# Instance norm over rows of 4096: ScalarE takes the first row's mean of each tile in place, VectorE the other three

One core of one Trainium2 chip. The metric is device time in microseconds (us) of one execution; lower is better.

## The reference

```python
x: float32 [256, 256, 4096], eps = 1e-5
mean = np.mean(x, axis=2, keepdims=True)
var = np.var(x, axis=2, keepdims=True)
return ((x - mean) / np.sqrt(var + eps)).astype(np.float32)
```

There are 65,536 rows of 4096. Every byte is read once and written once: 2147.5 MB of traffic in all. The input is drawn from a standard normal distribution.

## The kernel before

A tile holds 128 partitions x 4 rows x 4096. Three tile buffers rotate. SyncE (SP) issues all transfers on one queue, VectorE (V) and ScalarE (A) compute. Per tile SP does this:

```python
def store(s, t):                       # cut to its core
    take(S, done[s], K + 1)            # 4 applies by V, 1 by A
    S.dma_start(out=..., in_=X[s][:, :, :]).then_inc(stored[s], 16)
def load(s, t, wait=True):
    take(S, stored[s], 16)             # the buffer's last store has landed
    S.dma_start(out=X[s][:, :, :], in_=...).then_inc(loaded[s], 16)
...
for t in range(L0, L0 + BUFS):         # in a loop over rounds
    store(t % BUFS, ...)               # tile t
    load((t + 2) % BUFS, ...)          # tile t + 2
```

VectorE divides each row by 4096 in place and sums it, which gives the mean; ScalarE squares `x/4096 - mean` (scaled back) into a scratch tile in PSUM (an on-chip memory) and sums the squares, then takes a square root for each pair of rows; VectorE applies scale and bias to the rows, with ScalarE taking three quarters of the last row:

```python
for r in range(r0, r0 + k):                                    # V, line 87
    V.tensor_scalar(out=x[:, r, :], in0=x[:, r, :], scalar1=1.0 / d, scalar2=None,
        op0=ALU.mult, op1=ALU.add, accum_out=mean[s][:, r : r + 1]).then_inc(means, 1)
...
for r in range(r0, last + 1):                                  # A, line 137
    if own: A.wait_ge(own_a, own)
    ...                                # wait until V has counted r - r0 + 1 means
    mine(A.activation(out=junk, in_=x[:, r, :], func=AF.Square, bias=mean[s][:, c],
        scale=-float(d), accum_out=ss[s][:, c]))
    ...                                # after rows 1 and 3: square root of two rows, line 146
```

The first and the last tile are handled in halves of two rows, so one tile function runs 130 times: 126 whole tiles and 4 halves.

## Time and profile before

| | before |
|---|---|
| median of the first three runs | 4963.04 us (4962.19 to 4963.28) |
| span of the profiled run | 4960.2 us |
| VectorE busy, ScalarE busy | 66%, 49% |
| period of a tile in mid-run | 38.66 us |
| C: a tile's landing to the end of its last apply | 26.2 us |

The costliest groups on the page (line, engine, operation, out<-in, count | busy us, mean ns of one | idle time just before and what ended it):

```profile
L87 DVE TENSOR_SCALAR_CACHE_REDUCE x<-x 128x4096 f32<-128x4096 f32 x512 | 2232.3, 4416 | 1580.4 <-DMA x<-in_x_dram 1580.4
L137 ACT ACTIVATE junk<-x,mean 128x4096 f32<-128x4096 f32 x512 | 1883.1, 3678 | 2367.2 <-DVE x L87 2367.2
```

The row sum on VectorE (L87) is the largest block of engine work, and ScalarE is idle half of the time, mostly waiting for it. The 1580.4 us before L87 are VectorE waiting for loads.

### The profile page before, as it was taken

To read this page: it belongs to the slowest core of one execution; us is meant where nothing else is said; L and a number is where in the kernel's file an instruction comes from. 1 tells how busy PE (TensorE), PEld (TensorE's weight loads), DVE (VectorE), ACT (ScalarE), POOL (GpSimd) and SP (SyncE) were. 2 spreads that over 40 slices of the span, in tenths; PEclk is the share of its full clock that TensorE was granted. 3 is DMA by queue.
4 is the path that set the end of the run, shared out by engine and by line. 5 is a ranking of instruction groups with operands and counts; after the bars stand their busy time and mean duration, and the time that the engine had idled before them with its cause. 6 is when DMAs were issued, how large, how long until landed. Compare 5 with 4: busy or idle time off the path is not lost.

```text
span 4960.2 us, 5938 instructions
## 1 busy us (share of the span) xinstructions
DVE 3298.0 (66%) x2049; ACT 2407.7 (49%) x1412; POOL 0.2 (0%) x4
## 2 busy tenths in 40 slices
DVE  6666666666666666666666666666666666666666
ACT  4455444554445544455445544455444554445544
POOL 0000000000000000000000000000000000000000
DMA  9999999999999999999999999999999999999999
GB/s 422 431 435 433 431 435 433 432 437 432 432 438 432 433 437 432 433 437 432 435 435 432 436 434 431 438 433 431 438 433 432 438 432 433 438 432 433 438 432 405
DMA packets 37298, 2147.52 MB, mean 433 GB/s; under 512 B 4144, under 2 KB 4144, under 8 KB 4144
## 3 DMA queue, kind: packets, MB, share of 16 engines
q1 hardware_dynamic: 37296, 2147.50, 100.0%
q14 instruction: 2, 0.02, 0.0%
HBM read 1073.74 MB, written 1073.74 MB: 433 GB/s over the span
## 4 chain that ended last, share of the span: by engine, by line
DVE 62%; another core or an unknown queue 31%; issue 4%; DMA 2%; ACT 0%; DVEq 0%; ACTq 0%; SPq 0%
DVE x L87 44%; DVE x L112 17%; DMA x<-in_x_dram 1%; DVE nbias L100 1%; DMA out_dram<-x 1%; DVE rstd L98 1%; ACT junk L137 0%; DVEq L68 0%; DVEq L219 0%; ACT L146 0%; ACT std L146 0%; ACTq L68 0%; ACTq L67 0%; SPq L265 0%
## 5 line engine op out<-in xcount | busy, mean ns | idle before, releaser
L87 DVE TENSOR_SCALAR_CACHE_REDUCE x<-x 128x4096 f32<-128x4096 f32 x512 | 2232.3, 4416 | 1580.4 <-DMA x<-in_x_dram 1580.4
L137 ACT ACTIVATE junk<-x,mean 128x4096 f32<-128x4096 f32 x512 | 1883.1, 3678 | 2367.2 <-DVE x L87 2367.2
L112 DVE TENSOR_SCALAR x<-x,rstd,nbias 128x4096 f32<-128x4096 f32 (+1 forms) x512 | 1004.2, 2004 | 33.9 <-DVE nbias L100 29.3
L151 ACT ACTIVATE x<-x,nbias,rstd 128x3072 f32<-128x3072 f32 x130 | 383.2, 2948 | 146.2 <-DVEq L68 146.2
L137 ACT ACTIVATION_READ_ACCUMULATOR junk<-x,mean 128x1 f32 x512 | 95.5, 187 | 0.0
L146 ACT ACTIVATE std<-ss,eps_tile 128x2 f32<-128x2 f32 x256 | 75.6, 295 | 19.1
L98 DVE RECIPROCAL rstd<-std 128x2 f32<-128x2 f32 x256 | 40.7, 159 | 19.4 <-ACT std L146 19.4
L100 DVE SCALAR_TENSOR_TENSOR nbias<-mean,rstd 128x2 f32<-128x2 f32 x256 | 41.1, 161 | 8.9
L87 DVE DVE_READ_ACCUMULATOR x<-x 128x1 f32 x512 | 42.3, 83 | 0.0
L137 ACT ACT_TABLE_LOAD x1 | 1.3, 1283 | 1.2 <-DVE eps_tile L216 1.2
L146 ACT ACT_TABLE_LOAD x1 | 1.3, 1283 | 0.1
L216 DVE MEMSET eps_tile<- 128x1 f32 x1 | 0.1, 59 | 1.0 <-SPq L192 1.0
L251 POOL MEMSET const-bfloat16-1.0<- 128x1 bf16 x1 | 0.1, 101 | 0.0
L251 POOL MEMSET const-uint8-127<- 128x1 uint8 x1 | 0.1, 101 | 0.0
L251 POOL MEMSET const-float32-1.0<- 128x1 f32 x1 | 0.1, 99 | 0.0
L251 POOL MEMSET const-float32-0.0<- 128x1 f32 x1 | 0.1, 98 | 0.2 <-issue 0.2
## 6 DMA issues: line engine op xcount, KB each, us to landing
out_dram<-x SPq DMA_DIRECT2D x4, 4096.0 KB, 19.6
x<-in_x_dram SPq DMA_DIRECT2D x2, 4096.0 KB, 16.7
x<-in_x_dram SPq DMA_DIRECT2D x127, 50.3
out_dram<-x SPq DMA_DIRECT2D x126, 31.5
```

The source lines that it names most:

```text
L87: V.tensor_scalar(out=x[:, r, :], in0=x[:, r, :], scalar1=1.0 / d, scalar2=None, op0=ALU.mult, op1=ALU.add, accum_out=mean[s][:, r : r + 1 ...
L98: mine(V.reciprocal(out=rstd[s][:, c], in_=std[s][:, c]))
L100: mine(V.scalar_tensor_tensor(out=nbias[s][:, c], in0=mean[s][:, c], scalar=-1.0 / d, in1=rstd[s][:, c], op0=ALU.mult, op1=ALU.mult))
L112: V.tensor_scalar(out=x[:, r, f], in0=x[:, r, f], scalar1=rstd[s][:, c], scalar2=nbias[s][:, c], op0=ALU.mult, op1=ALU.add,).then_inc(dn, 1)
L137: mine(A.activation(out=junk, in_=x[:, r, :], func=AF.Square, bias=mean[s][:, c], scale=-float(d), accum_out=ss[s][:, c]))
L146: A.activation(out=std[s][:, c], in_=ss[s][:, c], func=AF.Sqrt, bias=eps_tile, scale=1.0 / d**3).then_inc(stds, 1)
L151: A.activation(out=x[:, last, :Q], in_=x[:, last, :Q], func=AF.Identity, bias=nbias[s][:, c], scale=rstd[s][:, c]).then_inc(dn, 1)
L216: V.memset(eps_tile, eps / d**2).then_inc(ready, 1)
L251: nc = _bacc.Bacc("TRN2", target_bir_lowering=False, num_devices=1)
```

## The change

The intent: take the first of the four row sums off VectorE and give it to ScalarE, which starts it as soon as the tile lands. A new semaphore passes the landing on.

```diff
+    landed = nc.alloc_semaphore("landed")
...                                                  # vector_tile
-        for r in range(r0, r0 + k):
+        V.sem_inc(landed, 1)
+        for r in range(r0 + 1, r0 + k):
             V.tensor_scalar(...)
...                                                  # scalar_tile
+        take(A, landed, 1)
+        mine(A.activation(
+            out=x[:, r0, :], in_=x[:, r0, :], func=AF.Copy, scale=1.0 / d, accum_out=mean[s][:, r0 : r0 + 1]
+        ))
         for r in range(r0, last + 1):
             c = slice(r, r + 1)
-            if own:
-                A.wait_ge(own_a, own)
+            A.wait_ge(own_a, own)
             if r == last:
-                take(A, means, k)
-            else:
-                A.wait_ge(means, r - r0 + 1)
+                take(A, means, k - 1)
+            elif r > r0:
+                A.wait_ge(means, r - r0)
```

## The prediction

> **What bounds the kernel now.** I read the page's busy shares first, then its DMA lines, then the timeline of two tiles in mid-run with the issuing queue, then the waits, then stretches of mid-run. The busy shares and the traffic:
>
> ```profile
> DVE 3298.0 (66%) x2049; ACT 2407.7 (49%) x1412; POOL 0.2 (0%) x4
> DMA  9999999999999999999999999999999999999999
> HBM read 1073.74 MB, written 1073.74 MB: 433 GB/s over the span
> x<-in_x_dram SPq DMA_DIRECT2D x127, 50.3
> out_dram<-x SPq DMA_DIRECT2D x126, 31.5
> ```
>
> No engine is busy all the time; the DMA engines are, in every slice. A tile is 128 x 4 x 4096 x 4 B = 8.39 MB, so one transfer at 433 GB/s is 19.4 us and a load plus a store is 38.75 us. The timeline shows how a tile's period is filled (start, duration, engine, line; excerpts of one tile and the start of the next):
>
> ```profile
> 2408.09 4.42 DVE L87 TENSOR_SCALAR_CACHE_REDUCE x<-x 128x4096 f32<-128x4096 f32 x1 [12.55 <-DMA x<-in_x_dram]
> 2412.56 3.68 ACT L137 ACTIVATE junk<-x,mean 128x4096 f32<-128x4096 f32 x1 [17.17 <-DVE x L87]
> ...
> 2425.85 4.74 DVE L112 TENSOR_SCALAR x<-x,rstd,nbias 128x4096 f32<-128x4096 f32 x2
> ...
> 2431.07 2.95 ACT L151 ACTIVATE x<-x,nbias,rstd 128x3072 f32<-128x3072 f32 x1 [1.14 <-DVEq L68]
> 2431.16 3.13 DVE L112 TENSOR_SCALAR x<-x,rstd,nbias 128x4096 f32<-128x4096 f32 x2 [0.30 <-DVE nbias L100]
> 2434.53 0.34 SPq L165 DMA_DIRECT2D out_dram<-x  x1
> 2435.11 0.35 SPq L170 DMA_DIRECT2D x<-in_x_dram  x1
> 2446.75 4.42 DVE L87 TENSOR_SCALAR_CACHE_REDUCE x<-x 128x4096 f32<-128x4096 f32 x1 [12.46 <-DMA x<-in_x_dram]
> ```
>
> The period is 2446.75 - 2408.09 = 38.66 us: the transfer time of a tile's 16.78 MB, at 434 GB/s. Work from a tile's landing to its last apply takes C = 2434.29 - 2408.09 = 26.2 us; then both engines stand still some 12.5 us until the next load lands. The waits say the same:
>
> ```profile
> DVE x L87 <- DMA x<-in_x_dram: 1580.4, 126, 13.2
> DVE rstd L98 <- ACT std L146: 19.4, 4, 5.8
> ```
>
> 1580.4 / 126 = 12.5 us per tile. Is that wait a latency or a queue? Landing times decide. The store issued at 2434.53 lands 31.5 us later though it needs 19.3 us, and the load issued just behind it takes 50.3 us. That is 12.2 us of an older load still ahead, then 19.3 us for the store, then about 19 us for the load itself: work in a queue that is served in order and is never empty. So DMA is the bound, with roughly 12 us of queued work in hand when the next pair is issued. The chain of waits gives VectorE 62% of the span, but it walks back through engine work wherever that joins a load's arrival; it doesn't weigh that the load would not have come sooner.
>
> **What the Trainium skill says.** (1) "DMA: Bandwidth & Descriptors", section "Where 436 GB/s comes from": 16 ports x 32 B x 850 MHz = 435 GB/s is the ceiling of the path to SBUF. The trace agrees: 433 over the span, 434 in mid-run, so there is under half a per cent left to win. (2) "SBUF — State Buffer", section "SBUF: two separate sides": engine accesses and DMA use different ports and don't slow each other. Stretches of mid-run, cut at the ends of the engines' work, agree (length, DVE busy, ACT busy, POOL busy, clock, DMA share, GB/s):
>
> ```profile
> 2408.00:2434.50 26.50, 25.79 (x16) 18.74 (x11) 0.00 (x0) 1.00 0.99 430
> 2434.50:2446.70 12.20, 0.00 (x0) 0.00 (x0) 0.00 (x0) 1.00 1.02 440
> ```
>
> 430 GB/s with engines at work and 440 without; records are credited packet by packet, so 2% over 12 us is no finding. (3) "ScalarE: Activation LUTs", section "What ACT_TABLE_LOAD costs": an activation with immediate scale and bias takes 186 ns + 0.833 ns per element, and each per-partition operand adds about 93 ns. The trace agrees: the square (one such operand, 4096) would be 3.69 us and takes 3.68; L151 (two, 3072) would be 2.93 and takes 2.95. (4) The same page, "Table sets: the hidden batching unit": copy is in every table set, so the new operation needs no further table load. The kernel before has two loads of 1.28 us in the whole run although three functions alternate, which fits; its trace has no copy.
>
> **The change, part by part.** Each of 130 calls (126 full tiles, and 2 tiles in halves) moves its first row from VectorE to ScalarE.
>
> Removed on VectorE: 130 of 512 instructions of L87. One advances the engine by 4.34 us (from the first row's start at 2408.09 to the second's at 2412.44, in the timeline), 4.36 us of busy time each (2232.3 / 512). 130 x 4.36 = 567 us, plus 130 accumulator reads of 83 ns = 11 us: busy falls from 3298 to about 2720 us (55%).
>
> Added on ScalarE: 130 copies with accumulation. Estimate from the page just named: 186 + 0.833 x 4096 = 3.60 us, plus the 0.187 us accumulator read of L137. 130 x 3.79 = 492 us: busy rises from 2408 to about 2900 us (58%). A semaphore increment on VectorE passes the landing on, about 0.1 us.
>
> Moved: the chain inside a tile. Count from the landing. ScalarE: copy 0.1 to 3.8 (accumulator read included; it overlaps its activation by 0.07); square of row 0 from 3.9 to 7.7, of row 1 from 7.9 to 11.7 (3.80 each with its read), first square root to 12.0, squares of rows 2 and 3 from 12.2 to 20.0, second root to 20.4 (0.295 each, gaps 0.03 to 0.2 as in the trace). VectorE: three rows end at 3 x 4.34 = 13.0; reciprocal and bias to 13.5; two applies in 4.17 to 17.6; then it waits for the second root until 20.5, some 2.5 to 3 us that it didn't wait before; reciprocal, bias and start 0.55; last applies 3.13. New C = 24.2 us, 2.0 us less than 26.2. ScalarE now carries the tile's chain.
>
> What is this worth? The pair store(t), load(t+2) is issued 2.0 us earlier after the landing, into a queue with 12.2 us of work in hand. It then has 14.2 us in hand. The load still lands one period of 38.6 us after the one before. On the path that sets the end: 124 x 0 = 0. The load's own wait, for the store of the tile before, doesn't bite: that store was issued one period earlier, at about 2395.9, and landed at 2427.4, which is 19.3 us after the landing at 2408.1, and the load will be asked for at 24.4.
>
> Start and end: the first tile's halves come free about 1 us sooner each (17.0 to 16.0), but two loads of 19.3 us fill the queue to about 41 us and the first half-store was issued at 31.5. At the end the last half-store was issued at 4941.7 and would come some 4 us sooner (2.0 from the last full tile, 1 from each half). From 4952 to the end only the slower DMA engines still move data, 84 GB/s over 8.2 us; those had a backlog at 4941.7 and don't end sooner for an earlier issue. At best, if slow and fast engines share a resource, the 0.06 of DMA share missing between 4908 and 4942 returns: 2 us. Sum: 0 to -2 us of 4963. I choose -1: **4962 us**.
>
> **The rivals.**
> *The loop is a latency loop.* A load's landing, C, and the issue of the load two tiles on close a ring: 26.2 + 0.6 + 50.3 = 77.1 us = two periods of 38.6. If 50.3 us were fixed, a shorter C would take 1.0 us off each period: 4963 - 124 = 4839 us, 2.5% faster. If even the 12.5 us wait were fixed, 124 x 2.0 = 248 us: 4715. For it speaks only the chain of waits and that the sum closes; against it, 50.3 is explained as queueing and 434 GB/s leaves no room under the 435.
> *ScalarE becomes the bound.* It has 2900 / 130 = 22.3 us of work in a 38.6 us period. C would have to grow to 38 us to starve the queue; even a copy at twice my estimate gives about 28. Time: 4962 still. Only a wait that I overlook, of over 14 us a tile, would cost time; then each further microsecond costs 124 us.
> *Contention.* ScalarE now also writes 2 MB more per tile to SBUF, VectorE as much less. If the 430 against 440 GB/s were contention after all, summed engine busy time barely changes (25.8 + 18.7 to 21.4 + 22.5 us a tile), so under 0.2%: 4953 to 4972.
>
> **Range and chances.** The three runs lie within 1.1 us. I add the end effect (to -2 us), a possible shift of the DMA rate with issue order (0.1%, 5 us, either way): 4955 to 4968. The latency loop gets 1.5%; something that starves the queue 1%.
>
> **What would show it.** Right: DVE busy near 2720 and ACT near 2900 us; copies of about 3.6 us, 130 of them; C near 24.2; VectorE's wait for loads up to about 14.5 us a tile (1580 to some 1820 us); a new wait of L98 for the square root, 2.5 to 3 us a tile, 310 to 370 us in all; landings later by 2 us (store 33.5, load 52.3) with the period at 38.6 and 433 GB/s. Wrong: landings unchanged with a shorter period (latency loop), or VectorE's load wait gone and GB/s below 430 (starved).

## The result

Ratios in this document are the mean time of one kernel's fast runs over that of the other's fast runs of the same rounds, so not quite the ratio of the medians that are quoted.

The changed kernel takes **4965.26 us** (4964.86 to 4965.61, 6 runs) against 4963.06 us (4961.5 to 4963.66, 6 runs): ratio 1.0005, 95% interval 0.9992 to 1.0018. The same within 2%, and inside the range of 4955 to 4968.

The page after: busy shares, DMA share in 40 slices, and issues with KB where known and us from issue to landing.

```profile
DVE 2745.6 (55%) x1789; ACT 2875.9 (58%) x1672; POOL 0.2 (0%) x4
DMA  9999999999999999999999999999999999999999
x<-in_x_dram SPq DMA_DIRECT2D x127, 52.9
out_dram<-x SPq DMA_DIRECT2D x126, 34.2
```

VectorE gave 552 us away and ScalarE took on 468 us, DMA is as full as it was, and both landing times grew by 2.6 to 2.7 us. The groups that changed (columns as above):

```profile
L89 DVE TENSOR_SCALAR_CACHE_REDUCE x<-x 128x4096 f32<-128x4096 f32 x382 | 1668.2, 4417 | 1906.0 <-DMA x<-in_x_dram 1906.0
L132 ACT ACTIVATE x<-x 128x4096 f32<-128x4096 f32 x130 | 470.1, 3616 | 1915.2 <-DVEq L69 1915.2
L100 DVE RECIPROCAL rstd<-std 128x2 f32<-128x2 f32 x256 | 41.7, 163 | 249.4 <-ACT std L151 249.4
```

130 sums left L89; 130 copies of 3.616 us stand at L132. VectorE's wait for loads rose from 1580.4 to 1906.0 us: the time saved in each tile reappears as waiting for the next one. ScalarE's 1915.2 us are the same wait, passed on by VectorE's semaphore increment. One tile in mid-run (start, duration, engine, line; cut):

```profile
2406.88 4.42 DVE L89 TENSOR_SCALAR_CACHE_REDUCE x<-x 128x4096 f32<-128x4096 f32 x1 [15.09 <-DMA x<-in_x_dram]
2406.89 3.62 ACT L132 ACTIVATE x<-x 128x4096 f32<-128x4096 f32 x1 [15.26 <-DVEq L69]
...
2410.63 3.68 ACT L142 ACTIVATE junk<-x,mean 128x4096 f32<-128x4096 f32 x1
...
2420.30 4.73 DVE L114 TENSOR_SCALAR x<-x,rstd,nbias 128x4096 f32<-128x4096 f32 x2
...
2426.32 0.29 ACT L151 ACTIVATE std<-ss,eps_tile 128x2 f32<-128x2 f32 x1
2426.75 0.17 DVE L100 RECIPROCAL rstd<-std 128x2 f32<-128x2 f32 x1 [1.73 <-ACT std L151]
...
2427.30 3.14 DVE L114 TENSOR_SCALAR x<-x,rstd,nbias 128x4096 f32<-128x4096 f32 x2 [0.19 <-DVE nbias L102]
...
2430.68 0.34 SPq L170 DMA_DIRECT2D out_dram<-x  x1
2431.26 0.35 SPq L175 DMA_DIRECT2D x<-in_x_dram  x1
2445.52 4.42 DVE L89 TENSOR_SCALAR_CACHE_REDUCE x<-x 128x4096 f32<-128x4096 f32 x1 [15.08 <-DMA x<-in_x_dram]
```

C is now 2430.44 - 2406.88 = 23.56 us, 2.6 us less. The period is 2445.52 - 2406.88 = 38.64 us: unchanged. The engines wait 15.1 us for each load where they waited 12.5. VectorE now waits for the second square root of each tile, which it didn't before.

### The profile page after: what moved, and what is told of

Same layout as the page of the kernel before. It is cut to its first block, busy times and chain, and to the rows that moved or that the text cites. A ratio compares the mean times of both kernels' runs of the same rounds, so it can differ in the third digit from the quotient of the medians.

```text
span 4963.8 us, 6069 instructions
## 1 busy us (share of the span) xinstructions
DVE 2745.6 (55%) x1789; ACT 2875.9 (58%) x1672; POOL 0.2 (0%) x4
## 4 chain that ended last, share of the span: by engine, by line
another core or an unknown queue 38%; ACT 37%; issue 16%; DVE 7%; DMA 1%; DVEq 0%; ACTq 0%; SPq 0%
ACT junk L142 26%; ACT x L132 10%; DVE x L114 6%; ACT std L151 1%; DMA x<-in_x_dram 1%; DVE nbias L102 1%; DVE rstd L100 0%; DVEq L69 0%; ACTq L69 0%; DVEq L224 0%; ACT L151 0%; ACT L132 0%; ACT x L156 0%; SPq L186 0%
## 5 line engine op out<-in xcount | busy, mean ns | idle before, releaser
L89 DVE TENSOR_SCALAR_CACHE_REDUCE x<-x 128x4096 f32<-128x4096 f32 x382 | 1668.2, 4417 | 1906.0 <-DMA x<-in_x_dram 1906.0
L132 ACT ACTIVATE x<-x 128x4096 f32<-128x4096 f32 x130 | 470.1, 3616 | 1915.2 <-DVEq L69 1915.2
L100 DVE RECIPROCAL rstd<-std 128x2 f32<-128x2 f32 x256 | 41.7, 163 | 249.4 <-ACT std L151 249.4
L89 DVE DVE_READ_ACCUMULATOR x<-x 128x1 f32 x382 | 31.6, 83 | 0.0
L132 ACT ACTIVATION_READ_ACCUMULATOR x<-x 128x1 f32 x130 | 24.2, 187 | 0.0
## 6 DMA issues: line engine op xcount, KB each, us to landing
x<-in_x_dram SPq DMA_DIRECT2D x127, 52.9
out_dram<-x SPq DMA_DIRECT2D x126, 34.2
```

The lines of the kernel that those rows point to most:

```text
L100: mine(V.reciprocal(out=rstd[s][:, c], in_=std[s][:, c]))
L132: mine(A.activation(out=x[:, r0, :], in_=x[:, r0, :], func=AF.Copy, scale=1.0 / d, accum_out=mean[s][:, r0 : r0 + 1]))
```

## The experiments

"Before" is always the kernel before, on the same chip, in the same rounds; its medians were 4962.06 us (9 runs on chip 12, beside no arithmetic, the changed kernel again, and one and three more squares), 4962.11 (7 runs on chip 1, of which two took 4999 and 5002; beside five more squares and less traffic), 4962.55 (7 runs on chip 1; two more squares and three rows loaded) and 4962.48 (11 runs on chip 12; the split store). So two more squares ran on another chip than one, three and the split.

**Theory A**: DMA is the bound, its queue is never empty, and C only sets how much work still stands in it when the next transfer is issued (the work in hand). **Rival B**: the landing time is a fixed latency, and a shorter C shortens the loop. **Rival C**: engine accesses slow the DMA.

### 1. No arithmetic at all

```diff
 # vector_tile, after the wait for the load
-        for r in range(r0, r0 + k):
-            V.tensor_scalar(...)
-        ...
+        V.sem_inc(dn, k + 1)
 # scalar_tile is never called
```

> Loads, stores and their semaphores alone, no arithmetic (wrong result on purpose). Theory A, full queue (DMA is the bound, and a tile's compute time C only sets how much work is queued): with C near 0 still 4950 to 4970 us, period 38.6 us, landings longer (about 58 us for load and store). Theory B, latency loop (landing time is fixed near 50.3 us): period (0.3 + 0.6 + 50.3) / 2 = 25.6 us, about 3300 us. Theory C, contention (engine accesses slow the DMA from 440 to 430 GB/s): 440 GB/s throughout, about 4885 us.

Measured: 4959.61 us (4958.65 to 4962.99, 5 runs) against 4962.06, ratio 0.9996 (0.9983 to 1.001). (It counted as correct because the input is nearly normalised already; it is a copy and no solution.) The page:

```profile
DVE 0.1 (0%) x1; POOL 0.2 (0%) x4
HBM read 1073.74 MB, written 1073.74 MB: 433 GB/s over the span
x<-in_x_dram SPq DMA_DIRECT2D x127, 57.7
out_dram<-x SPq DMA_DIRECT2D x126, 57.6
```

With C at nothing the time stays and the landing of a load grows from 50.3 to 57.7 us and that of a store from 31.5 to 57.6: the landing time is queueing. (A load's grows less because SP now waits, before it issues one, for the store of the tile before: 2413.3 us in 129 waits.) B (3300 us) and C (4885 us) fall. Against C speaks a stretch of the changed kernel too: it shows 439 GB/s with the engines at work (2406.80 to 2430.70 us) and 425 without (2430.70 to 2445.50), the reverse of the 430 and 440 in the prediction. All 5700 us of engine work in the kernel before cost some 2.5 us of span, within the spread of the runs. So a change on the engines alone has no more than about that to gain here while all this traffic goes through this queue.

### 2. The changed kernel again

> The changed kernel once more, as a control on this chip. If the 2.2 us that it lost are the kernel's own, 4964.5 to 4966 against 4961.5 to 4964 for the kernel before; if they were chance of a chip or a day, the two overlap.

Measured: 4965.32 us (4964.72 to 4966.14, 5 runs) against 4962.06 (4961.19 to 4963.24). The two groups don't overlap, as in the first comparison, though the 95% interval of the ratio, 0.9992 to 1.002, includes 1. The loss of 2 to 3 us (some 0.06%) is small but comes back in a second set of runs, so it seems to belong to the kernel. More on it below.

### 3. Longer C: one, three and five more squares per tile

In each whole tile ScalarE repeats the square of row 0 into PSUM `n` times; the last one is overwritten with the same value, so the result stays right.

```diff
+        for _ in range(n if k == K else 0):
+            A.wait_ge(own_a, own)
+            mine(A.activation(out=junk, in_=x[:, r0, :], func=AF.Square, bias=mean[s][:, r0 : r0 + 1],
+                 scale=-float(d), accum_out=ss[s][:, r0 : r0 + 1]))
```

> The changed kernel with one more square of row 0 into PSUM per full tile: C from 23.6 to 27.4 us, a little over the kernel before (26.2), ScalarE's writes to SBUF unchanged. Theory A: same, 4960 to 4968. For the lost 2.2 us: if more work in hand costs them, about 4963 or less, as before; if ScalarE's added writes to SBUF cost them, still about 4965. Theory B: 1.9 us per period more, about 5205.

> Three more squares of row 0 per full tile: C about 35.1 us, 11.5 us more, still under the period of 38.6. Theory A: same, 4958 to 4970, and the engines' wait for loads falls from 15.1 to about 3.5 us a tile. Theory B: 5.8 us per period more, about 5690.

> Five more squares of row 0 per full tile: C about 42.8 us, over the 38.6 us period. Theory A: the queue runs dry and the engines set the pace: 126 x 42.8 us plus about 90 us at start and end, 5470 to 5500 us, DMA share near 0.9, no wait for loads left. Theory B: 9.6 us per period more, about 6175.

Measured: one more (C 27.4 us) 4964.23 us (4963.54 to 4975.24, 5 runs, four of them under 4965.5), ratio 1.001. Three more (C 35.1) **5055.88** us (5053.63 to 5069.38, 5 runs), ratio 1.0188 (1.0174 to 1.0202). Five more 5439.68 us (2 runs), ratio 1.0934 (1.0854 to 1.1014; the two slow runs of before are in its base).

The first is as A expects. The second is a miss: A promised 4958 to 4970 for every C under the period of 38.6, and B its 5690. The third is in the regime that A named, but 30 us under the range: the period is 42.44 us between store issues, not 42.8, because ScalarE goes straight from one tile into the next. The DMA queue's line (packets, MB, share of the 16 engines' span that packets took) and the traffic, with three more:

```profile
q1 hardware_dynamic: 37296, 2147.50, 99.3%
HBM read 1073.74 MB, written 1073.74 MB: 424 GB/s over the span
```

and with five more, with the busy shares:

```profile
DVE 2745.4 (50%) x1789; ACT 5256.6 (97%) x2932; POOL 0.2 (0%) x4
q1 hardware_dynamic: 37296, 2147.50, 93.2%
```

With five, ScalarE is the bound (97%) and the queue stands empty for part of each tile. With three, the queue is empty for only 0.7% of the span and still moves 2% less. The packet records of the trace say how. A packet of 64 KB takes 2.418 us in the median in all these kernels, but some take longer:

```
                      packets over 2.6 us   their excess over
kernel                (of 32,384)           2.418 us, per engine
before                  101                    3.4 us
changed                 150                    4.1
no arithmetic           114                    3.6
one more                155                    5.0
three more             1892                   67.2
five more              2503                  100.9
```

The long packets with three and five more lie almost all 16 to 24 us after a store's issue, where the queue turns from the store to the next load. The few of the kernel before lie mostly 6 to 10 us after the issue, where it turns from a load to the store; nearly half of them (46 of 101) fall in the first 250 us, and one after 1250. For the profiled run with three more (5069.38 us, 107 us over before) the sum nearly closes: 0.7% of 5067.6 us are 35 us of empty queue, and the long packets add 67.2 - 3.4 = 64 us. So the loss with three has two parts, and the slower packets are the larger.

The trace shows a second thing that A had overlooked. A load's landing is when the last of its 16 DMA engines is done. With three more, in one tile 15 engines reported between 2413.02 and 2413.38 us and the sixteenth at 2415.86. SP issued the next store at 2412.50, "3.4 us ahead of the landing", but the last packets of those 15 engines ended at 2412.7 to 2413.0, and their next ones started only at 2413.3. What the landing shows in hand is the last engine's work; the first engines have less, by the spread between them.

### 4. Where does the loss begin

Two more squares, and two with one of half a row:

```diff
-        for _ in range(n if k == K else 0):
+        for w in (d, d) if k == K else ():          # plus2h: (d, d, d // 2)
             ...                                      # the same on [:, :w]
```

> The changed kernel with two more squares of row 0: C about 31.2 us. Theory D (a queue with work has no cost, but it runs dry some 3 to 4 us before its last load's landing is seen, so the cliff lies near C = 34 us and not at the period of 38.6): 4960 to 4968 us, period 38.7. Theory E (each added us of C costs something all along; the line through one and three added squares, 12 us per us of C): about 5010.

> Two more squares of row 0 and one of half a row: C about 33.3 us, just under the cliff that theory D puts near 34. Theory D: 4960 to 4975 us. Theory E: about 5035.

Measured: C 31.2 us: 5013.52 us (5012.17 to 5016.23, 4 runs), ratio 1.0104 (1.0087 to 1.012). C 33.3 us: 5015.15 us (5011.0 to 5019.03, 4 runs), ratio 1.0109 (1.0092 to 1.0125). Theory D, which put the cliff near 34, falls. E has the number for two but misses the next by 20 us: it is no line. It is a step of 1% between C = 27.4 and 31.2, flat up to 33.3, and then more. The queue's line and the traffic with two more:

```profile
q1 hardware_dynamic: 37296, 2147.50, 100.0%
HBM read 1073.74 MB, written 1073.74 MB: 428 GB/s over the span
```

Packets fill the engines' whole span, so hardly anything waits; they are slower: 1546 over 2.6 us with 49.9 us of excess per engine, which is about the 51 us lost. A quarter of them lie where the queue turns from load to store, three quarters where it turns from store to load. So the step is not an empty queue but slower packets at its turns.

The traces also show what goes with the step. When SP issues a store, each of the 16 engines still has a part of the load before it to finish. The 16 increments of that load's landing give how long, sorted from the first engine to the last (us, medians of mid-run):

```
kernel             first    8th    15th   last
before               4.8    5.2    11.9   12.2
changed              9.9   11.2    14.3   14.8
one more             5.7    7.0    10.8   10.9
two more             1.6    1.9     6.7    7.5
two and a half       1.6    1.8     4.7    5.3
three more           1.5    1.8     2.0    4.4
```

The kernels without loss leave the first engine more than a packet's 2.418 us of work, the slower ones leave less than that to half of the engines or more. The last column, which the prediction counted, falls without such a step. This fits the flat part up to C = 33.3 us too, where the first half of the engines has as much left as at 31.2. But this is only a match of numbers: no run tests it by itself, and it is not shown to be the cause.

### 5. The same C, with the store in two halves

```diff
+        S.wait_ge(done[s], half)
+        S.dma_start(out=...[:, :half, :], in_=X[s][:, :half, :]).then_inc(stored[s], 16)
         take(S, done[s], K + 1)
-        S.dma_start(out=..., in_=X[s][:, :, :]).then_inc(stored[s], 16)
+        S.dma_start(out=...[:, half:, :], in_=X[s][:, half:, :]).then_inc(stored[s], 16)
```

> The kernel with two added squares (C 31.2 us, 5013 us), its store cut in two: rows 0 and 1 go out as soon as they are ready, at about 24.0 us, rows 2 and 3 at 31.2. Engine work and C are unchanged. Theory F (what costs is too little work in hand: the DMA engines that are ahead run dry, all start again together, and packets stretch where the queue turns from stores to loads): some 14 us in hand at the first half-store as in the two kernels without loss, so 4960 to 4975 us, and hardly any packets over 2.6 us. Theory G (ScalarE's added work slows the DMA by contention): 5013 us still.

Measured: 4971.83, 5013.56, 5017.64, 4970.84, 5015.41, 4969.09 us. Ratio 1.007 (1.0036 to 1.0103), but that mean hides two times, some 4970 and some 5015, mixed on one chip. G falls as it stands: with the same engine work half of the runs lose hardly anything. F falls too as it stands: 14 us in hand at the first half-store don't keep the other half out of the slow mode. The profile fell in a run of 4971.83 us; there the first engine had 8.1 us left at the first half-store, and 310 of 16,256 packets of 64 KB took over 2.6 us. The two runs of 4999 and 5002 us of the kernel before hint that it can fall into something like it too; no profile of those exists.

So with the split store, at C near 31 us, the DMA engines run in one of two modes. That more work in hand makes the better one possible is likely but not shown: the unsplit kernel ran in the slow mode in all 4 runs, but on another chip, and the split also cut the packets of the stores from 64 to 32 KB. What decides between the modes stays open.

### 6. Less traffic: is the shorter C real?

If DMA hides the gain, less DMA must show it. Both kernels store only half of each tile's first row (wrong; 9.44 MB per tile in place of 16.78):

```diff
-        S.dma_start(out=rows_of(out_t, t), in_=X[s][:, :, :])
+        S.dma_start(out=rows_of(out_t, t)[:, 0, : d // 2], in_=X[s][:, 0, : d // 2])
```

> The kernel before, which stores only half of each tile's first row (wrong result on purpose): 9.44 MB per tile instead of 16.78, 21.7 us at 434 GB/s, under C. Theory A: the engines become the bound, period near C = 26.2, 126 x 26.3 plus 95 = about 3400 us.

> The changed kernel with the same reduced store. Theory A: period near C = 23.6, 126 x 23.7 plus 85 = about 3065 us, so 10% faster than the kernel before with the same store: the change pays as soon as DMA does not bind. If the shorter C were an illusion of the trace (or the DMA bound both), the two would be equal.

Measured: 3384.2 us and **3134.74** us (4 runs each, both within 0.6 us): the change gains 7.4%, not the expected 10%. The waits of the two, before first:

```profile
DVE x L87 <- DMA x<-in_x_dram: 20.2, 2, 12.1
```

```profile
DVE x L89 <- DMA x<-in_x_dram: 94.4, 64, 12.3
```

The kernel before waits for loads only at the start; the changed one waits again in every second tile. Its store issues come 24.06 us apart on average, which is the loop of rival B: C 23.56 + issue 0.83 + landing 23.6 = 48.0 us, two periods. With little traffic the queue is short, the landing is mostly transfer, and the loop binds. A load that lands sooner should free it, so in a second pair only three of four rows are loaded in the loop:

```diff
+        rows = slice(0, K if isinstance(t, int) else K - 1)
-        S.dma_start(out=X[s][:, :, :], in_=rows_of(x_t, t)).then_inc(loaded[s], 16)
+        S.dma_start(out=X[s][:, rows, :], in_=rows_of(x_t, t)[:, rows, :]).then_inc(loaded[s], 16)
```

> The kernel before with the reduced store and, in the loop, three of four rows loaded (wrong result on purpose): some 16.9 us of transfer per tile. It was engine-bound with the reduced store alone (period 26.03 us), so no change: 3375 to 3390 us.

> The changed kernel with the same. If it missed its 3065 us with the reduced store because the loop of landing, C and issue bound it there (23.6 + 0.8 + 23.6 = two periods of 24.0), a load that lands about 5 us sooner frees it: period 23.3 to 23.5, 3030 to 3050 us. If the engines themselves need the 24.06 us period: 3135 as before.

Measured: 3383.79 us and 3037.56 us (4 runs each), both in their ranges. The changed kernel no longer waits for loads after the start:

```profile
DVE x L89 <- DMA x<-in_x_dram: 24.7, 2, 12.5
```

3037.56 / 3383.79 = 0.898: 10% faster. The change does to the engines what it was meant to do.

### 7. The 2 to 3 us that were lost

Explanations were at hand: more work in the queue costs them, or ScalarE's added writes to SBUF (the on-chip memory that holds the tiles) do. The copy without arithmetic has the most work in the queue and the lowest median, so the first falls. One more square, with the added writes but less work in hand than before, takes 4964.23 us, between the two kernels; that settles nothing. What the traces show is where the time is. From load to load, taken from the timelines and landings:

```
                 mean period    first 12 tiles   mid-run   last tiles   from 38.64 to 38.73
before             38.70 us      38.7 to 39.6     38.64      38.73       after some 115 tiles
changed            38.73         38.6 to 39.4     38.64      38.73       after some 67 tiles
changed, again     38.73         38.6 to 39.9     38.64      38.73       after some 63 tiles
one more square    38.72         38.6 to 39.7     38.64      38.73       after some 73 tiles
no arithmetic      38.68         38.7 to 39.8     38.64      38.64       never
```

A step of 0.09 us per tile comes some 50 tiles earlier: 50 x 0.09 = 4.5 us, less a lead of 1.2 us that the changed kernel had in mid-run. The changed kernel's second profile steps early too (it has a disturbed stretch of up to 38.83 us just before), and the copy without arithmetic never does. After the step one DMA engine falls behind all the others by that much per tile: in the changed kernel the last increment of a landing trails the one before it by 0.4 us in mid-run and by 5.6 us at the end. At the end (stretch, its length, busy times, clock, DMA share, GB/s) before

```profile
4952.00:4960.20 8.20, 0.00 (x0) 0.00 (x0) 0.00 (x0) 1.00 0.20 84
```

and after

```profile
4952.00:4963.80 11.80, 0.00 (x0) 0.00 (x0) 0.00 (x0) 1.00 0.15 67
```

the first engines are done near 4952 us in both kernels. The fifteenth is done at 4958.1 us before and 4956.8 after, the last at 4959.2 before and 4962.7 after. Counted by the other fifteen engines, the two kernels end about level (the second profile of the changed kernel has 4958.2 and 4963.1 us). Why that engine slows, and why sooner with the change, is open.

## Why the prediction was right, and where it was not

- **The bound: right.** DMA sets the time; the copy without arithmetic shows that at most some 2.5 us of 4963 depend on the engines.
- **Costs: right.** VectorE 2745.6 us (said about 2720), ScalarE 2875.9 (about 2900), a copy 3.616 us (3.60 from the formula of the skill's page). The page of the changed kernel has two table loads, as before.
- **The tile's chain: right in kind, a little long.** C 23.56 us (24.2). VectorE's new wait for the square root is 249.4 us in all, under the 310 to 370 that were said. The mis-sized term is the spacing on ScalarE: the second square follows the first by 3.83 us (4.0 was put down), and the third starts 0.20 us after the first root's start and overlaps it (0.5 was put down), so that the second root ends 19.7 us after the landing and not 20.4.
- **Where the gain goes: right.** Landings 34.2 and 52.9 us (33.5 and 52.3), load wait 15.1 us a tile (14.5), period unchanged.
- **Start and end: wrong in sign.** -1 us was said for the sum of start and end; it is +2.2, from the step in the period above, which the sum had no term for. The range held because it left 5 us either way for a shift of the DMA rate; that it held for the loss is in part luck, since no cause for a loss was given.
- **Rival "latency loop": rightly refused**, though for this traffic only: it binds as soon as less traffic goes through the queue (section 6).
- **Rival "ScalarE becomes the bound": its threshold was wrong.** The text said that only a wait of over 14 us a tile would cost time. Added to the changed kernel's C of 23.56 us, 3.8 us cost nothing, but 7.7 us cost 51 us against the kernel before and 11.5 us cost 94. The step that failed is "work in hand is the wait for the landing": the landing is the slowest of 16 engines, and the others have less in hand (in the kernel before 12.2 us by the landing, but 4.8 on the first engine). Packets at the queue's turns become slower before the queue is empty: with 7.7 us more they still fill 100.0% of the span.

## What to carry to other kernels

Before moving work between engines, ask what the engines wait for: where a transfer's landing time exceeds its own length by the work queued ahead, and traffic is at its ceiling, a shorter chain only becomes a longer wait. Test it with a kernel that only moves the data; here it gave the floor for changes on the engines. And don't spend the whole wait: here a chain that ended some 8 us ahead of the next landing already cost 1%, when half of the DMA engines had under 2 us of work left.

## What the Trainium skill lacked or had wrong

- "DMA: Bandwidth & Descriptors" (section "Where 436 GB/s comes from") says that for transfers between HBM and SBUF the HBM side, about 358 GB/s, binds. This program, on one core, held 434 GB/s in mid-run, reads and writes together; the page's 435 GB/s is the ceiling that fits (its own single-core measurement, 425 GB/s, says as much). "Perfetto Trace Analysis" (section "Engine Utilization") takes 358 GB/s as 100%, but says that a core alone reaches about 120% of it; the trace agrees (434 / 358 = 121%).
- The same DMA page has nothing on packets that become slower where one queue turns from stores to loads: 1546 of 32,384 packets of 64 KB took over 2.6 us in place of 2.418 (1% of the time) at C = 31.2 us, 101 in the kernel before.
- The same page says that each engine posts its own increment. It lacks what this means for a full queue: the engines of one store finished up to 10.7 us apart at the end of the changed kernel (8.5 before), so the landing overstates the work that the first engines have left.
- "ScalarE: Activation LUTs" gives the cost of an activation well (3.60 against 3.616 us) but not that of the separate read of the accumulator, 0.187 us each here.
